# Strassen's derived weight blocks: added up by accumulating transfers from GpSimd, not subtracted by VectorE

## The chip, the cores and the metric

The kernel runs on one core of a Trainium2 chip. A core has five engines that run side by side, each through its own fixed list of instructions: TensorE (PE, matrix products; its weight loads are listed as PEld), VectorE (DVE), ScalarE (ACT), GpSimd (POOL) and SyncE (SP), which here does nothing but issue transfers. Transfers run on 16 DMA engines that all queues of the core share. An instruction that has to wait for a semaphore holds up all that stand behind it on its engine. The metric is the device time of one execution in microseconds (us); lower is better.

## The reference

One layer of a streaming-encoder block on x of 256 tokens by 2048 channels, all in float32. Three sublayers follow one another, each with a layer norm and a conditioning (shift, scale, gate) that is computed from a vector c:

```python
y = _swiglu(modulate(x, 0), ffn1_w13[l], ffn1_w2[l])
x = _layer_norm(ALPHA * x + FFN_WEIGHT * gate[:, 0, None, :] * y, ln_g[l, 0], ln_b[l, 0])
...
x = _layer_norm(ALPHA * x + gate[:, 1, None, :] * y, ln_g[l, 1], ln_b[l, 1])
y = _swiglu(modulate(x, 2), ffn2_w13[l], ffn2_w2[l])
x = _layer_norm(ALPHA * x + FFN_WEIGHT * gate[:, 2, None, :] * y, ln_g[l, 2], ln_b[l, 2])
```

The middle sublayer (an mLSTM beside a gated linear recurrence) is left out here: the change touches only the third, whose SwiGLU is

```python
g, v = jnp.split(u @ w13, 2, axis=-1)
return (jax.nn.silu(g) * v) @ w2
```

with u 256 by 2048, w13 2048 by 2 x 5632 and w2 5632 by 2048.

## The kernel before

**Products in three parts.** A float32 operand is split into a high part (rounded to the matrix unit's format, a cast on ScalarE, L99) and a low part (the rest, a subtraction on VectorE, L101). A product is high x high + low weights x high + high x low, three matmuls (L305, L306, L307) into the same PSUM bank. A weight tile is 128 x 2048 float32, 1 MB; it is loaded by SyncE into one of four buffers of the tag `raw`, and its two parts go into one of three `hi` and three `lo` buffers. In the profile the tiles are called by their first letters: `rw` is the loaded tile of `w2`, `hw` and `lw` its parts; `rf`, `hf`, `lf` the same of `w13`.

**Blocks.** The hidden columns of the feed-forward come in 11 blocks of 512; a block needs `g` (gate) and `v` (value) for two halves t of 128 tokens, over 2048 channels in four tiles of 512. Blocks 4 to 9 of the second feed-forward are *mixed*: two of the four channel tiles (0 and 1) of both `g` and `v` are computed by Strassen's method in Winograd's form. The 2 x 2 blocks of the one operand are token halves by channel tiles, those of the other are the four weight tiles r[0] (`g`, tile 0), r[1] (`v`, tile 0), r[2] (`g`, tile 1) and r[3] (`v`, tile 1). Seven products q1 to q7 take the place of eight, at the price of derived blocks: four of the tokens (`token_sums`, made once), and four of the weights, made in every block by VectorE in place, L880, L881, L882 and L891: r[0] = r[1] - r[0], r[1] = r[3] - r[1], r[3] = r[3] - r[0], r[2] = r[2] - r[3]. Tiles 2 and 3 are multiplied plainly (`plain`).

**The order in a mixed block** is that of `mixed`: q1 (r[0] as loaded), a `w2` tile of the group before, q2 (r[2] as loaded), plain tile 2 of `g`, q3 (r[3] as loaded), a `w2` tile, q6 (r[3] derived), plain tile 3 of `g`, q7 (r[1] derived), a `w2` tile, q5 (r[0] derived), a `w2` tile, q4 (r[2] derived), and the plain tiles of `v`. In the profile `hq` and `lq` are the parts of r[0] to r[3], `m` the PSUM banks of q1, q5, q6 and q7, `fg` and `fv` those of `g` and `v`, `py` those of the `w2` products, `b` the tiles r[0] to r[3] (`b6_3` is r[3] of block 6).

**Buffers.** r[0] and r[1] of every block live in two fixed tiles (tags `scb` and `gate`); r[2] and r[3] take two of the four `raw` buffers, and so the tile that is loaded next into the buffer of r[3] has to wait until r[3] is read for the last time. In blocks 4 to 8 that next tile is the third `w2` tile of the block (`rw22_4_1` in block 6), and in block 9 the fourth. The four tiles of the next block are fetched by `fetch_w` (L835) as their places come free.

**What sets the order.** A scheduler lays the program out on each engine once, when it is built; on the chip every engine keeps to its list. `mov_t` (L298 to L308) issues the products of one token half, `split` (L92) the two parts of a tile.

Of the kernel before, what the change touches and what calls it, by code (L numbers as in the profile page):

```python
# [15 lines left out]
ALU = mybir.AluOpType  # L16
# [38 lines left out]
def block_kernel(ctx: ExitStack, tc: tile.TileContext, a: dict, out: bass.AP):  # L55
    nc = tc.nc
# [16 lines left out]
    def bank(name):  # L73
        return psp.tile([P, 512], F32, tag="ps", name=name)

    def raw_tile(name):
        return wp.tile([P, 2048], F32, tag="raw", bufs=4, name=name)
# [14 lines left out]
    def split(tile, act, low):  # L92

        raw, name, into = tile
        hi, lo = into() if into else [wp.tile([P, 2048], F32R, tag=w, bufs=3, name=w[0] + name) for w in ("hi", "lo")]
        step = 512 if fine[0] else 2048
        cols = [slice(c, c + step) for c in range(0, 2048, step)]
        for w in cols:
            act.copy(cut(hi, w), like(raw[:, w], hi))  # L99
        for w in cols:  # L100
            low.tensor_sub(cut(lo, w), like(raw[:, w], lo), cut(hi, w).bitcast(F32))  # L101
        return hi, lo

    def load_w(src, name, into=None):

        return split(load(src, name, into), nc.scalar, nc.vector)
# [191 lines left out]
    def mov_t(ps, hl, acth, actl, k0, t, first, last, te=nc.tensor, part=slice(0, 512)):  # L298

        hi, lo = hl  # L300
        tk = slice(t * P, (t + 1) * P)
        for j in range(4):
            w = slice(j * 512 + part.start, j * 512 + part.stop)
            o = like(ps[:, part], hi)
            te.matmul(o, acth[:, k0 + j, tk], cut(hi, w), start=first and j == 0, stop=False)  # L305
            te.matmul(o, acth[:, k0 + j, tk], cut(lo, w), start=False, stop=False)  # L306
            mm = te.matmul(o, actl[:, k0 + j, tk], cut(hi, w), start=False, stop=last and j == 3)  # L307
        return mm  # L308
# [7 lines left out]
    def tile_done(mm):  # L316

        for p in pend:
            p[0] -= 1
        while pend and pend[0][0] <= 0:  # L320
            with tc.issue_after(mm.ins):
                pend.pop(0)[1]()
# [260 lines left out]
    def ffn(s, w13, w2, start, following=None):  # L583
# [221 lines left out]
        def token_sums():  # L805

            home = big.tile([P, 2, KT, P], F32R, tag="x", name="sums")
            ah = raw_tile("usum").rearrange("p (k b) -> p k b", k=8)
            nc.vector.tensor_add(ah, uh[:, 0:8, :].bitcast(F32), ul[:, 0:8, :].bitcast(F32))
            a11, a12, a21, a22 = (ah[:, k:k + 4, t * P:(t + 1) * P] for t in range(NT) for k in (0, 4))
            ss = raw_tile("ssum").rearrange("p (k b) -> p k b", k=KT)
            s1, s2, s3, s4 = (ss[:, 4 * i:4 * i + 4, :] for i in range(4))
            nc.vector.tensor_add(s1, a21, a22)
            nc.vector.tensor_sub(s2, s1, a11)  # L820
            nc.vector.tensor_sub(s3, a11, a21)
            nc.vector.tensor_sub(s4, a12, s2)
            sh, sl = home[:, 0], home[:, 1]
            nc.scalar.copy(sh, ss)
            nc.vector.tensor_sub(sl, ss, sh.bitcast(F32))
            parts[:] = sh, sl
# [11 lines left out]
        def mixed(b, ws, more):  # L838

            sh, sl = parts
            r = [held.pop((b, j)) for j in range(4)]  # L850

            def parted(j, nm):
                return split((r[j], f"{nm}{s}_{b}", None), nc.scalar, nc.vector)

            def product(ps, hl, acth, actl, k0, t, first, last):
                tile_done(mov_t(ps, hl, acth, actl, k0, t, first, last))

            def plain(pss, k, at, first, last):
                tile_k = load_w(w13[8 * b + at + k], f"f{s}_{b}{at}{k}")
                for t in range(NT):  # L860
                    mm = mov_t(pss[t], tile_k, uh, ul, 4 * k, t, first[t], last[t])
                tile_done(mm)

            def part_bank(nm):
                return bank(f"{nm}{s}_{b}")

            def half_tile(tag, nm):
                return sm.tile([P, 512], F32, tag=tag, bufs=2, name=f"{nm}{s}{b}")

            sub = nc.vector.tensor_sub  # L870
            add = nc.vector.tensor_add
            p1 = part_bank("m1")
            product(p1, parted(0, "q1"), uh, ul, 0, 0, True, True)
            next(ws)()
            g = [part_bank("fg0"), part_bank("fg1")]
            v = [part_bank("fv0"), None]
            product(g[0], parted(2, "q2"), uh, ul, 4, 0, True, False)
            plain(g, 2, 0, (False, True), (False, False))
            product(v[0], parted(3, "q3"), sh, sl, 12, 0, True, False)
            sub(r[0], r[1], r[0])  # L880
            sub(r[1], r[3], r[1])  # L881
            sub(r[3], r[3], r[0])  # L882
            w0 = half_tile("u", "wa")
            nc.scalar.copy(w0, p1)
            next(ws)()
            p6 = part_bank("m6")
            product(p6, parted(3, "q6"), sh, sl, 4, 0, True, True)
            z0 = half_tile("gy", "za")
            add(z0, w0, p6)
            plain(g, 3, 0, (False, False), (True, False))  # L890
            sub(r[2], r[2], r[3])  # L891
            if more:
                fetch_w(b + 1, 3)
            p7 = part_bank("m7")
            product(p7, parted(1, "q7"), sh, sl, 8, 0, True, True)
            z1 = half_tile("gy", "zb")
            add(z1, z0, p7)
            next(ws)()
            if more:
                fetch_w(b + 1, 1)  # L900
            p5 = part_bank("m5")
            product(p5, parted(0, "q5"), sh, sl, 0, 0, True, True)
            add(z0, z0, p5)
            add(w0, w0, g[0])
            nc.scalar.activation(w0, w0, AF.Silu)
            next(ws)()
            if more:
                fetch_w(b + 1, 0)
            product(g[1], parted(2, "q4"), uh, ul, 4, 1, False, True)
            w1 = half_tile("u", "wb")  # L910
            add(w1, z1, g[1])
            nc.scalar.activation(w1, w1, AF.Silu)
            add(z1, z1, p5)
            v[1] = part_bank("fv1")
            plain(v, 2, 4, (False, True), (False, False))
            if more:
                fetch_w(b + 1, 2)
            plain(v, 3, 4, (False, False), (True, True))
            for t, (w, z) in enumerate(((w0, z0), (w1, z1))):
                add(z, z, v[t])  # L920
                nc.vector.tensor_mul(w, w, z)
            if 4 * b // GRP not in hts:
                new_h(4 * b // GRP)
            later(3, lambda: turn(b, [w0, w1]))
# [524 lines left out]
```

## Time and profile before

| | us |
|---|---|
| median of three runs (lowest, highest) | 1889.85 (1889.34, 1890.07) |
| the profiled execution | 1891.85 |
| its span in the profile | 1890.1 |
| granted TensorE clock over it | 0.995 |
| stretch of the six mixed blocks | about 1376 to 1757 |

The profile shows one execution. Its page gives the busy time of each engine, the chain of work that ended last, groups of instructions by source line with what ended the idle time before them, and the transfers. Other views used below: the busy time of the engines in stretches of the span, the timeline of one engine (start, duration, engine, line, operation, tiles, count, and in brackets the idle time before it with what ended it), and one tile's instructions. A row of SPq is the issue of a transfer; how long the transfer takes until it has landed stands in the view of the transfers.

### The profile page before, as it was taken

How to read it: one execution, taken by the hardware profiler on the slowest of the kernel's cores; microseconds unless marked ns; L12 is line 12 of the kernel's file. 1: busy time of each engine (PE TensorE's matmuls, PEld its weight loads, DVE VectorE, ACT ScalarE, POOL GpSimd, SP SyncE). 2: the span in 40 equal slices, each digit the busy share in tenths (PEclk: the TensorE clock that was granted, in tenths of full speed). 3: DMA queues.
4: the chain of work that ended last, by engine and by line, in shares of the span. 5: the costliest groups of instructions: out<-in, count | busy, mean ns of one | idle time of the engine just before them, and what ended most of it. 6: DMA issues, size and time to landing. Idle time of an engine off the chain costs nothing.

```text
span 1890.1 us, 21168 instructions
## 1 busy us (share of the span) xinstructions
PE 1852.1 (98%) x8483; PEld 1526.3 (81%) x8483; DVE 1541.1 (82%) x1454; ACT 883.8 (47%) x817; POOL 43.1 (2%) x64
## 2 busy tenths in 40 slices
PE   6999999999999999999999999999999999999997
PEld 4888888888888888688888876888888888888886
DVE  7899978888877988898898886677677788778757
ACT  5633434444433335756734346434454454445440
POOL 0000000000000000000000121000000000000000
PEclk8999999999999999999999999999999999999999
DMA  9989887888988897597689575577845654564762
GB/s 363 350 326 361 339 305 292 312 328 335 358 340 336 332 352 267 185 367 283 223 334 363 219 304 224 226 292 264 311 159 197 223 200 178 201 222 156 270 224 85
DMA packets 73490, 520.05 MB, mean 275 GB/s; under 512 B 8576, under 2 KB 8752, under 8 KB 11056
## 3 DMA queue, kind: packets, MB, share of 16 engines
q1 hardware_dynamic: 71136, 511.74, 71.6%
q10 hardware_dynamic: 1728, 3.80, 0.6%
q0 software_dynamic: 528, 3.17, 0.5%
q8 instruction: 66, 1.08, 0.2%
q14 instruction: 32, 0.26, 0.0%
HBM read 514.46 MB, written 4.22 MB: 274 GB/s over the span
## 4 chain that ended last, share of the span: by engine, by line
PE 86%; DVE 6%; ACT 3%; DMA 3%; issue 2%; POOL 0%; DVEq 0%; SPq 0%; ACTq 0%
PE py L306 6%; PE py L305 6%; PE py L307 6%; PE rp L694 5%; PE rp L695 5%; PE fv L305 5%; PE fv L306 5%; PE rp L696 5%; PE fv L307 5%; PE fg L305 4%; PE fg L306 4%; PE fg L307 4%; PE pj L294 4%; PE tl L305 3%; PE tl L306 3%; PE tl L307 3%
## 5 line engine op out<-in xcount | busy, mean ns | idle before, releaser
L189 DVE CUSTOM_DVE_ANT_0 ada<-ada,scb,badac 128x2048 f32<-128x2048 f32 x142 | 332.9, 2345 | 43.8 <-DMA ada<-in_w_ada 43.7
L99 ACT CAST hw<-rw 128x2048 fp32r<-128x2048 f32 x80 | 153.2, 1915 | 180.4 <-PE py L307 79.0
L101 DVE TENSOR_TENSOR lw<-rw,hw 128x2048 fp32r<-128x2048 f32 x80 | 183.0, 2288 | 55.0 <-ACT hw L99 54.9
L307 PE MATMUL py<-hw,htl 128*128 128x512 f32 x512 | 198.9, 389 | 0.0
L306 PE MATMUL py<-lw,hth 128*128 128x512 f32 x512 | 198.9, 389 | 0.0
L99 ACT CAST hra<-rra 128x2048 fp32r<-128x2048 f32 x63 | 120.6, 1916 | 161.8 <-PE rp L696 122.6
L305 PE MATMUL py<-hw,hth 128*128 128x512 f32 x512 | 195.8, 390 | 0.0
L695 PE MATMUL rp<-lra,u 128*128 128x512 f32 x448 | 174.2, 389 | 1.1 <-DVE lra L101 1.1
L696 PE MATMUL rp<-hra,u 128*128 128x512 f32 x448 | 173.6, 389 | 0.0
L694 PE MATMUL rp<-hra,u 128*128 128x512 f32 x448 | 170.7, 392 | 2.4 <-ACT u L262 1.7
L101 DVE TENSOR_TENSOR lra<-rra,hra 128x2048 fp32r<-128x2048 f32 x63 | 144.0, 2286 | 27.7 <-ACT hra L99 27.6
L101 DVE TENSOR_TENSOR lq<-b,hq 128x2048 fp32r<-128x2048 f32 x42 | 96.1, 2288 | 55.0 <-ACT hq L99 55.0
L99 ACT CAST hq<-b 128x2048 fp32r<-128x2048 f32 x42 | 80.4, 1913 | 118.3 <-PE py L307 62.7
L294 PE MATMUL pj<-u,hs 128*128 128x512 f32 x512 | 122.8, 392 | 0.7 <-ACT hs L99 0.7
L307 PEld LDWEIGHTS py<-hw,htl 128*128 128x128 f32 x512 | 96.1, 188 | 20.1
L305 PEld LDWEIGHTS py<-hw,hth 128*128 128x128 f32 x512 | 96.1, 188 | 20.0
L306 PEld LDWEIGHTS py<-lw,hth 128*128 128x128 f32 x512 | 96.1, 188 | 19.6
L294 PEld LDWEIGHTS pj<-u,hs 128*128 128x128 f32 x512 | 94.2, 188 | 19.5 <-ACT hs L99 1.1
L694 PEld LDWEIGHTS rp<-hra,u 128*128 128x128 f32 x448 | 84.0, 188 | 21.1 <-ACT u L262 2.4
L695 PEld LDWEIGHTS rp<-lra,u 128*128 128x128 f32 x448 | 84.1, 188 | 18.5 <-DVE lra L101 1.5
L99 ACT CAST hfv<-rfv 128x2048 fp32r<-128x2048 f32 x31 | 59.3, 1917 | 84.6 <-PE fg L307 63.2
L696 PEld LDWEIGHTS rp<-hra,u 128*128 128x128 f32 x448 | 84.1, 188 | 17.6
(470 smaller groups left out, 4048.8 us busy)
## 6 DMA issues: line engine op xcount, KB each, us to landing
ada<-in_w_ada SPq DMA_DIRECT2D x142, 1024.0 KB, 5.3
rw<-in_w SPq DMA_DIRECT2D x80, 1024.0 KB, 5.3
rra<-in_w_r SPq DMA_DIRECT2D x64, 1024.0 KB, 5.0
rs<-in_w_s SPq DMA_DIRECT2D x32, 1024.0 KB, 6.4
rfg<-in_w SPq DMA_DIRECT2D x31, 1024.0 KB, 5.3
rfv<-in_w SPq DMA_DIRECT2D x31, 1024.0 KB, 5.5
b<-in_w SPq DMA_DIRECT2D x24, 1024.0 KB, 4.8
rf<-in_w SPq DMA_DIRECT2D x24, 1024.0 KB, 4.8
```

Source lines behind the costliest of these rows:

```text
L99: act.copy(cut(hi, w), like(raw[:, w], hi))
L101: low.tensor_sub(cut(lo, w), like(raw[:, w], lo), cut(hi, w).bitcast(F32))
L189: vec.tensor_tensor_reduce(raw, raw, scb, 1.0, badac[:, s, j, kt:kt + 1], ALU.mult, ALU.add, adac[:, s, j, kt:kt + 1])
L294: nc.tensor.matmul(ps, hi[:, w], u2[:, k].rearrange("p w b -> p (w b)"), start=k == 0, stop=False)
L305: te.matmul(o, acth[:, k0 + j, tk], cut(hi, w), start=first and j == 0, stop=False)
L306: te.matmul(o, acth[:, k0 + j, tk], cut(lo, w), start=False, stop=False)
L307: mm = te.matmul(o, actl[:, k0 + j, tk], cut(hi, w), start=False, stop=last and j == 3)
L694: nc.tensor.matmul(pss[t], uh[:, k0 + j, tk], hi[:, w], start=a0 and j == j0, stop=False)
L695: nc.tensor.matmul(pss[t], uh[:, k0 + j, tk], lo[:, w], start=False, stop=False)
L696: mm = nc.tensor.matmul(pss[t], ul[:, k0 + j, tk], hi[:, w], start=False, stop=a1 and j == j0 + nj - 1)
```

## The change

The four derived weight blocks become sums, made in place by transfers that GpSimd issues and that add what they carry to what is in the destination:

- r[0] += the `v` tile 0, read again from memory (before it was r[1] - r[0], with the other sign of r[0]);
- r[1] += the `v` tile 1, read again from memory;
- r[3] += r[0], from one on-chip tile to another;
- r[2] += r[3], likewise.

The transfers into r[0] and r[1] are issued behind q1's product, that into r[3] behind q3, that into r[2] behind the plain tile 3 of `g`: where the subtractions of r[0], r[1] and r[3] stood together behind q3, they now stand apart. To fit the sums, the signs in `token_sums` and in three of the combinations `z0`, `z1` and `w1` change.

```diff
@@ token_sums
-            nc.vector.tensor_add(s1, a21, a22)
+            nc.vector.tensor_sub(s1, a22, a21)
             nc.vector.tensor_sub(s2, s1, a11)
-            nc.vector.tensor_sub(s3, a11, a21)
-            nc.vector.tensor_sub(s4, a12, s2)
+            nc.vector.tensor_add(s3, a11, a21)
+            nc.vector.tensor_add(s4, a12, s2)
@@ mixed
+            def plus(j, src):
+                nc.gpsimd.dma_start(r[j], src, accum_op=ALU.add)
+
             p1 = part_bank("m1")
             product(p1, parted(0, "q1"), uh, ul, 0, 0, True, True)
+            plus(0, w13[8 * b + 4])
+            plus(1, w13[8 * b + 5])
             next(ws)()
...
             product(v[0], parted(3, "q3"), sh, sl, 12, 0, True, False)
-            sub(r[0], r[1], r[0])
-            sub(r[1], r[3], r[1])
-            sub(r[3], r[3], r[0])
+            plus(3, r[0])
...
             plain(g, 3, 0, (False, False), (True, False))
-            sub(r[2], r[2], r[3])
+            plus(2, r[3])
...
-            add(z0, z0, p5)
+            sub(z0, p5, z0)
...
-            add(w1, z1, g[1])
+            sub(w1, g[1], z1)
...
-            add(z1, z1, p5)
+            sub(z1, z1, p5)
```

On VectorE, in block 6 around the derivation of r[3] and r[2], there stood before (`lq32_6` and `lq62_6` are the low parts of q3 and q6, `lw22_5_0` that of a `w2` tile, `htl2` a part of the hidden activations):

```order
L101 TENSOR_TENSOR lq32_6_10706<-b6_3_10397,hq32_6_10705 128x2048
L882 TENSOR_TENSOR b6_3_10397<-b6_3_10397,b6_0_10504 128x2048
L101 TENSOR_TENSOR lw22_5_0_10729<-rw22_5_0_10726,hw22_5_0_10728 128x2048
L638 TENSOR_TENSOR htl2_10181<-th50_10661,hth2_10180 128x4x128
L638 TENSOR_TENSOR htl2_10181<-th51_10668,hth2_10180 128x4x128
L891 TENSOR_TENSOR b6_2_10557<-b6_2_10557,b6_3_10397 128x2048
L101 TENSOR_TENSOR lq62_6_10760<-b6_3_10397,hq62_6_10759 128x2048
```

and now:

```order
L101 TENSOR_TENSOR lq32_6_10708<-b6_3_10397,hq32_6_10707 128x2048
L101 TENSOR_TENSOR lw22_5_0_10729<-rw22_5_0_10726,hw22_5_0_10728 128x2048
L638 TENSOR_TENSOR htl2_10181<-th50_10663,hth2_10180 128x4x128
L638 TENSOR_TENSOR htl2_10181<-th51_10670,hth2_10180 128x4x128
L101 TENSOR_TENSOR lq62_6_10760<-b6_3_10397,hq62_6_10759 128x2048
```

L882 and L891 are gone, and the rest has kept its order; so have ScalarE's rows. GpSimd, which had nothing between the normalisation ahead of this feed-forward and the gate at its end, now has four rows a block; here from the last of that normalisation to block 4 (`ven11` and `rsn11` belong to it), and then those of block 6 with the first of block 7 (in brackets the semaphores that each waits for: DMAHW are transfers issued by SyncE, DMASW those issued by GpSimd):

```order
L124 TENSOR_TENSOR rsp11_8368<-vep11_8366,mhalf_80 128x1 [waits Pool_49]
L874 DMA b4_1_9781<-in_w13_2 128x2048 [waits DMAHW0_49,DMASW3_49]
L124 TENSOR_SCALAR ven11_8396<-tot11_8392 128x1 [waits DVE_49]
L124 TENSOR_TENSOR rsn11_8398<-ven11_8396,mhalf_80 128x1 [waits Pool_49]
L874 DMA b4_0_9775<-in_w13_2 128x2048 [waits DMAHW3_49,DVE_49]
...
L874 DMA b6_1_10450<-in_w13_2 128x2048 [waits DMAHW2_49,DMASW0_49,DVE_49]
L874 DMA b6_0_10504<-in_w13_2 128x2048 [waits DMAHW4_49,DVE_49]
L874 DMA b6_3_10397<-b6_0_10504 128x2048 [waits DMAHW3_49,DMAHW5_49,DMASW7_49,DMAHW7_49,DMASW5_49,DVE_49]
L874 DMA b6_2_10557<-b6_3_10397 128x2048 [waits DMAHW5_49,DMAHW6_49,DMAHW1_49,DMASW6_49]
L874 DMA b7_1_10861<-in_w13_2 128x2048 [waits DMAHW6_49,DMASW4_49,DVE_49]
```

The accumulate into r[1] comes first in every block, and in block 4 it stands ahead of the two small operations of the normalisation. That into r[3] waits for the one into r[0] (DMASW5) and for the q3 split (DVE), that into r[2] for the one into r[3] (DMASW6). On SyncE the rows of block 6 that load the next block's r[3], two `w2` tiles and what follows stood so before:

```order
L835 DMA b7_3_10808<-in_w13_2 128x2048 [waits DMAHW1_49,DVE_49]
L89 DMA rw22_4_1_10831<-in_w2_2 128x2048 [waits DMAHW4_49,DVE_49]
L89 DMA rw22_5_1_10883<-in_w2_2 128x2048 [waits DMAHW5_49,DMAHW2_49,DVE_49]
L835 DMA b7_1_10861<-in_w13_2 128x2048 [waits DVE_49]
L89 DMA rf2_642_10938<-in_w13_2 128x2048 [waits DMAHW4_49,DVE_49]
```

and now:

```order
L835 DMA b7_3_10808<-in_w13_2 128x2048 [waits DMAHW1_49,DVE_49]
L89 DMA rw22_4_1_10831<-in_w2_2 128x2048 [waits DMASW7_49,DMAHW4_49,DMASW6_49,DVE_49]
L89 DMA rw22_5_1_10883<-in_w2_2 128x2048 [waits DMAHW5_49,DMAHW2_49,DVE_49]
L835 DMA b7_1_10861<-in_w13_2 128x2048 [waits DMASW4_49,DVE_49]
L89 DMA rf2_642_10938<-in_w13_2 128x2048 [waits DMAHW4_49,DVE_49]
```

The order is the same, but `rw22_4_1`, which takes the buffer of `b6_3`, now also waits for the accumulates into r[3] (DMASW6) and r[2] (DMASW7), since the latter reads r[3].

## The prediction

> **What bounds the kernel now.** I read the page's first part, then the busy time by stretch over the part of the program that the change touches, and then the timelines of single engines inside one block of it.
>
> ```profile
> span 1890.1 us, 21168 instructions
> PE 1852.1 (98%) x8483; PEld 1526.3 (81%) x8483; DVE 1541.1 (82%) x1454; ACT 883.8 (47%) x817; POOL 43.1 (2%) x64
> ...
> PE 86%; DVE 6%; ACT 3%; DMA 3%; issue 2%; POOL 0%; DVEq 0%; SPq 0%; ACTq 0%
> ```
>
> TensorE is busy 98% of the span and holds 86% of the chain that ended last. That is an average; the change lies in six blocks, so I asked for four stretches of one block's length (columns: stretch, length, PE, PEld, DVE, ACT and POOL busy, clock, DMA share, GB/s).
>
> ```profile
> 1442.50:1506.00 63.50, 63.50 (x286) 52.68 (x285) 52.33 (x36) 31.23 (x20) 0.00 (x0) 1.00 0.54 198
> 1506.00:1569.40 63.40, 63.40 (x286) 52.56 (x285) 52.16 (x36) 31.23 (x20) 0.00 (x0) 1.00 0.54 200
> ...
> sum 253.80, PE 253.80 PEld 210.48 DVE 208.84 ACT 124.94 POOL 0.00; mean PE 63.45 PEld 52.62 DVE 52.21 ACT 31.23 POOL 0.00
> ```
>
> TensorE has no idle time at all here (253.80 of 253.80 us, at granted clock 1.00). VectorE is busy 52.21 of 63.45 us in a block, so it waits 11 us. So nothing that makes VectorE lighter can shorten these blocks. The question is only whether the sums come in time.
>
> **What is removed.** Four subtractions a block (columns: line, engine, tiles, count, total and mean):
>
> ```profile
> L882 DVE TENSOR_TENSOR b<-b,b 128x2048 f32<-128x2048 f32 x6 | 13.8, 2292 | 0.2
> L880 DVE TENSOR_TENSOR b<-b,b 128x2048 f32<-128x2048 f32 x6 | 13.7, 2285 | 0.0
> L881 DVE TENSOR_TENSOR b<-b,b 128x2048 f32<-128x2048 f32 x6 | 13.7, 2282 | 0.0
> L891 DVE TENSOR_TENSOR b<-b,b 128x2048 f32<-128x2048 f32 x6 | 13.7, 2280 | 0.0
> ```
>
> That is 54.9 us of VectorE in 24 instructions, 9.1 us a block. It lies wholly beside TensorE's work: worth 0. The operations whose sign changes keep engine, size and number: 0.
>
> **What is added.** 24 accumulating transfers of 1 MB, issued by GpSimd, which is idle here (0.00 in the stretches). No accumulating transfer stands in this trace, so its price has to be bounded. These rows are near (tile, queue, count, size, median us from issue to landing; the `gateb` group's landing is the last line):
>
> ```profile
> b<-in_w SPq DMA_DIRECT2D x20, 1024.0 KB, 4.8
> ...
> xb<-xd SPq DMA_DIRECT2D x1, 2048.0 KB, 7.8
> ...
> xd<-x SPq DMA_DIRECT2D x1, 2048.0 KB, 11.3
> ...
> gate<-line POOLq DMA_DIRECT2D x1, 1024.0 KB, 8.2
> ...
> DMA to landing us min/median/max: 5.0/5.0/5.0
> ```
> ```profile
> 921.79 0.33 SPq L188 DMA_DIRECT2D ada<-in_w_ada  x1
> ...
> 922.18 0.56 POOL L212 DMA_DIRECT2D gate<-line  x1 [1.66 <-DMA line<-grow]
> ```
>
> A plain load of 1 MB lands in 4.8 us and one of 2 MB in 7.8: 1.8 fixed and 3.0 per MB. The same MB issued by GpSimd took 5.0 (`gateb`), 0.2 more. The one into `gate`, issued 0.4 us after a load (921.79, 922.18), took 8.2, and 2 MB stored among loads took 11.3: company adds 3.2 to 3.5. An accumulate must fetch the destination as well as the source. From below it costs **5.0** (the second fetch hides); with 2 MB fetched **8.0** alone and **11.3** in company; from above **14.3**, if the two fetches and the write follow one another (1.8 + 3 x 3.0 + 0.2) and company adds 3.3. I take the two fetches as the work, so the 2 MB row is nearest: 8.0 alone.
>
> The Trainium skill, "Collectives: The Full Stack", section "The bandwidth ceiling: the fold count and why AG ≠ RS ≠ AR", says that an add inside the transfer is slow for its second source read, at half the rate, and not for the adding. By it the sum below would stand; without the second read (5.0) there would be no stall. No run here shows an accumulate yet.
>
> **Where each of the four lands.** Block 6, VectorE first, then ScalarE, SyncE's queue and TensorE:
>
> ```profile
> 1505.05 2.28 DVE L101 TENSOR_TENSOR lq<-b,hq 128x2048 fp32r<-128x2048 f32 x1
> ...
> 1522.99 2.29 DVE L101 TENSOR_TENSOR lq<-b,hq 128x2048 fp32r<-128x2048 f32 x1 [1.65 <-ACT hq L99]
> 1525.31 2.29 DVE L882 TENSOR_TENSOR b<-b,b 128x2048 f32<-128x2048 f32 x1
> 1527.52 2.28 DVE L101 TENSOR_TENSOR lw<-rw,hw 128x2048 fp32r<-128x2048 f32 x1
> ...
> 1533.12 2.28 DVE L101 TENSOR_TENSOR lq<-b,hq 128x2048 fp32r<-128x2048 f32 x1
> ```
> ```profile
> 1530.15 1.92 ACT L99 CAST hq<-b 128x2048 fp32r<-128x2048 f32 x1 [3.03 <-PE fg L307]
> ...
> 1541.44 1.92 ACT L99 CAST hw<-rw 128x2048 fp32r<-128x2048 f32 x1 [1.26 <-PE m L307]
> ...
> 1554.64 1.91 ACT L99 CAST hq<-b 128x2048 fp32r<-128x2048 f32 x1 [3.53 <-PE py L307]
> ```
> ```profile
> 1479.07 0.33 SPq L835 DMA_DIRECT2D b<-in_w  x1
> ...
> 1529.83 0.33 SPq L835 DMA_DIRECT2D b<-in_w  x1
> 1535.43 2.53 SPq L89 DMA_DIRECT2D rw<-in_w  x2
> ```
> ```profile
> 1538.75 0.39 PE L306 MATMUL m<-lq,sums 128*128 128x512 f32 x1
> ...
> 1549.40 0.39 PE L306 MATMUL py<-lw,hth 128*128 128x512 f32 x1
> ...
> 1557.56 0.39 PE L306 MATMUL py<-lw,hth 128*128 128x512 f32 x1
> ```
>
> *Into `r[0]`*: may start when the q1 split has read it (1505.05 + 2.28 = 1507.33) and is wanted by the next accumulate at 1525.28: 17.9 us, enough even at 14.3. *Into `r[1]`*: its load was issued at 1479.07, tens of us early: hidden.
>
> *Into `r[3]`*: starts when the q3 split has read it, at 1522.99 + 2.29 = 1525.28. VectorE was done with L882 2.3 us later, and the split q6 then waited for TensorE until 1530.15 anyway. The first matmul that needs q6's low half starts at 1538.75. Split high 1.92 and low 2.28 lie between, so the sum must have landed by 1534.55: **9.3 us after its start**. In those us SyncE also loads the next block's `r[3]` (1529.83, some 2 us earlier once L882 no longer precedes the `lw` that frees its buffer), so I take 8.0 + 2.0 = 10.0, between alone and in full company: 0.7 late.
>
> *Into `r[2]`*: starts when the one before has landed. Its own reader, q4's split at 1554.64, has time. But the `w2` tile that SyncE loads at 1535.43 goes into the buffer of `r[3]`, and now also waits until `r[3]` has been read by this transfer. That load lands 4.8 later, is split (1.92 and 2.28), and its low half is used at 1549.40: it must be issued by 1540.40, **15.1 us after 1525.28**. Behind it in SyncE's order stand one more `w2` tile, needed 8.2 us later (1557.56), and the next block's loads; all have more time than this one. With SyncE waiting, nothing runs beside this transfer: 8.0. The two together are 18.0: **2.9 us late**, the 0.7 included. TensorE's order is fixed, so it waits out the whole of it, and the next block's q3 split is tied to TensorE's buffers (the chain `ACT hq <- PE`), so that every block pays anew.
>
> Block 4 has less room:
>
> ```profile
> 1396.97 2.29 DVE L101 TENSOR_TENSOR lq<-b,hq 128x2048 fp32r<-128x2048 f32 x1 [3.14 <-ACT hq L99]
> ...
> 1422.48 0.39 PE L306 MATMUL py<-lw,hth 128*128 128x512 f32 x1
> ```
>
> From 1399.26 to 1422.48 are 23.22 us, against 24.12 in block 6: 0.9 less, so 3.8 late. In block 9 the buffer of `r[3]` goes to the later `w2` tile, 8.2 us more room, and only the 0.7 is left.
>
> One accumulate stands early: that into block 4's `r[1]` is put on GpSimd ahead of two small operations of the normalisation before it.
>
> ```profile
> 1157.83 0.33 SPq L835 DMA_DIRECT2D b<-in_w  x1
> ...
> DMA to landing us min/median/max: 4.8/4.8/4.8
> ```
> ```profile
> 1166.75 0.62 POOL L124 TENSOR_SCALAR ven<-tot 128x1 f32<-128x1 f32 x1 [5.34 <-DVE nbn L124]
> ```
>
> Its tile lands at 1162.63, and the operation behind it starts at 1166.75: 4.1 us of cover, worth 0; without it the normalisation of half the tokens would move by what is missing.
>
> **The sum.** 3.8 + 4 x 2.9 + 0.7 = **16.1 us**. The profiled execution took 1891.85 us (span 1890.1), so it would take 1908.0; the median of the runs is 2.0 lower, so **1906 us** there.
>
> **The rivals.** *Hidden (not slower).* The pair has 15.1 us a block. If both transfers land within 7.5 us each, TensorE never waits, and the time stays 1890. For it: the 5.0 us of `gateb`; and the share that I gave to company is a choice. Against it: 2 MB alone took 7.8. The Trainium skill, "DMA: Bandwidth & Descriptors", section "Anatomy of one DMA — SWDGE (gpsimd) path", gives 2.0 us plus the bytes at 436 GB/s for one issued by GpSimd: 6.8 us, an estimate for 2 MB, 13.6 for the pair, and so no stall. The trace's GpSimd MB took 5.0 where that rule makes 4.4. Chance 20%.
>
> *Slow accumulate.* At 14.3 each the pair takes 28.6: 13.5 late in a block, 14.4 in block 4; block 9 waits 5.3 (28.6 against 15.1 + 8.2): 14.4 + 4 x 13.5 + 5.3 = 73.7, so 1964. For it: the transfers already fill 0.54 of the DMA engines, 34 of 63.45 us, and four accumulates at 6 us of fetching make that 58, so that company is the rule. Against it: only one load falls into the critical 18 us. From 22 us for the pair (7 a block) I count it here. Chance 27%, half of it beyond 1964.
>
> *Faster.* It would need idle time of TensorE that VectorE makes, and the stretches have none: 3%. That the subtractions simply stay is excluded by the built order, which has 24 fewer VectorE rows and 24 more of GpSimd.
>
> **How the numbers follow.** The forecast, a pair between 15.7 and 22 us, has 50%: 1894 to 1927. The range goes down to 1889, which takes in the hidden case, and up to 1970 for the slow one; some 12% is left above it and 4% below. A measurement of this kernel can tell about 0.2% (3.8 us) from no change. The hidden case falls within it except for its edges: same 0.17, faster 0.03, slower 0.80.
>
> **What would show it.** Right: DVE busy falls by 55 us, TensorE gets idle time only in blocks 4 to 9, ended by `lw` L101 and in front of `py`; SyncE's queue waits before that `rw` load for the accumulate into `r[2]`; accumulates that land in 8 to 10 us. Wrong: landings below 7.5 and PE still without idle time (hidden), or landings of 14 and waits in front of `m` from q6 as long as 5 us (slow). A wait of `ven` on GpSimd near 1166 would show the early accumulate mispriced. Landings over 18 us would break the cover of the one into `r[0]` too.

## The result, and the profile after

The changed kernel takes 1904.32 us (median of 4 runs, 1902.31 to 1906.52), the kernel before 1889.96 on the same chip (1889.34 to 1893.35): a ratio of 1.0073, 95% interval 1.0055 to 1.0090. It is slower by 14.4 us; 1906 was forecast. Its profiled execution took 1906.52 us, with a span of 1904.6.

The head of the page of the changed kernel, with the chain's shares by engine:

```profile
span 1904.6 us, 21239 instructions
PE 1858.7 (98%) x8483; PEld 1526.7 (80%) x8483; DVE 1488.5 (78%) x1430; ACT 882.6 (46%) x817; POOL 61.6 (3%) x88
...
PE 67%; DMA 13%; issue 9%; DVE 6%; ACT 4%; POOL 0%; DVEq 0%; SPq 0%; ACTq 0%; POOLq 0%
```

VectorE lost 24 instructions and 52.6 us, and nothing came of it: the span grew. Transfers now hold 13% of the chain that ended last, against 3%. The next view has the busy time of each engine from one q3 split's end to the next, in five blocks (columns as in the prediction's view by stretch):

```profile
1398.98:1464.84 65.86, 63.67 (x281) 51.57 (x280) 42.21 (x29) 29.66 (x18) 3.43 (x5) 1.00 0.83 255
1464.84:1530.29 65.45, 64.32 (x285) 52.48 (x284) 43.41 (x31) 30.90 (x22) 3.43 (x5) 1.00 0.83 257
1530.29:1596.96 66.67, 64.39 (x285) 52.39 (x284) 43.40 (x31) 30.87 (x21) 3.41 (x4) 1.00 0.82 252
1596.96:1664.20 67.24, 64.58 (x285) 52.35 (x284) 43.41 (x31) 30.88 (x21) 3.42 (x5) 1.00 0.81 250
1664.20:1730.50 66.30, 64.39 (x285) 52.48 (x284) 43.40 (x31) 30.87 (x21) 3.43 (x5) 1.00 0.83 254
```

A block took 63.45 us before (253.80 over four). Against 63.45 the five are longer by 2.4, 2.0, 3.2, 3.8 and 2.8: 14.3 of the span's 14.5 us. TensorE, which had no idle time there, now waits; VectorE is down to 43 us a block, and the DMA engines' share is up from 0.54 to 0.82. What TensorE waited for in the six blocks (columns: line, releaser, us in all, times, longest):

```profile
PE py L306 <- DVE lw L101: 6.1, 5, 1.6
PE m L305 <- ACT hq L99: 3.3, 4, 1.1
PE py L305 <- ACT hw L99: 0.7, 1, 0.7
```

Two places. The waits in front of `py`, 6.8 us, are those of the forecast. The 3.3 in front of `m` are not: they belong to the next block's q1. And the landing times in the same part of the program (tile, queue, count, size, median us):

```profile
rw<-in_w SPq DMA_DIRECT2D x23, 1024.0 KB, 7.8
rf<-in_w SPq DMA_DIRECT2D x23, 1024.0 KB, 5.0
b<-in_w SPq DMA_DIRECT2D x20, 1024.0 KB, 9.0
b<-b POOLq DMA_DIRECT2D x12, 1024.0 KB, 7.9
b<-in_w POOLq DMA_DIRECT2D x11, 1024.0 KB, 10.2
```

An accumulate from one tile into another (`b<-b`: into `r[3]` and `r[2]`) takes 7.9 us, one from memory (`b<-in_w` on GpSimd's queue: into `r[0]` and `r[1]`) 10.2. The plain loads beside them grew from 4.8 to 7.8 (`rw`) and 9.0 (`b`).

Block 6 again, in the order GpSimd, SyncE's queue, ScalarE, TensorE:

```profile
1530.29 0.85 POOL L874 DMA_DIRECT2D b<-b  x1 [13.89 <-DVE lq L101]
1538.49 0.85 POOL L874 DMA_DIRECT2D b<-b  x1 [7.36 <-DMA b<-b]
1557.95 0.85 POOL L874 DMA_DIRECT2D b<-in_w  x1 [18.61 <-DMA b<-in_w]
```
```profile
1532.74 0.33 SPq L835 DMA_DIRECT2D b<-in_w  x1
1545.68 1.58 SPq L89 DMA_DIRECT2D rw<-in_w  x2
1548.17 0.33 SPq L835 DMA_DIRECT2D b<-in_w  x1
...
1566.44 0.33 SPq L89 DMA_DIRECT2D rf<-in_w  x1
```
```profile
1538.31 1.91 ACT L99 CAST hq<-b 128x2048 fp32r<-128x2048 f32 x1 [6.46 <-DMA b<-b]
...
1552.54 1.90 ACT L99 CAST hw<-rw 128x2048 fp32r<-128x2048 f32 x1 [7.64 <-DMA rw<-in_w]
...
1574.89 1.91 ACT L99 CAST hf<-rf 128x2048 fp32r<-128x2048 f32 x1 [8.12 <-DMA rf<-in_w]
```
```profile
1554.49 0.73 PE L305 MATMUL py<-hw,hth 128*128 128x512 f32 x2 [0.67 <-ACT hw L99]
1556.82 0.50 PE L306 MATMUL py<-lw,hth 128*128 128x512 f32 x1 [1.59 <-DVE lw L101]
```

Read downwards: the q3 split ends at 1529.99, the accumulate into `r[3]` is issued at 1530.29, and q6's split starts at 1538.31, 8.3 us after the split's end and in time. The one into `r[2]` goes out at 1538.49, and SyncE, which stands in front of the third `w2` tile because that takes the buffer of `r[3]`, may go on at 1545.68: 15.7 us after the q3 split, 0.6 past the limit of 15.1. Then three loads leave together (two `rw`, one `b`), and the first takes 6.8 us to land, not 4.8 (its split starts 6.9 us after the issue). TensorE waits 2.26 us (0.67 + 1.59).

Block 6 is the worst of the five at this place. All of them, in us (how much later TensorE is behind a place than ahead of it, by the starts of the same matmuls before and after):

| block | third `w2` load issued after the q3 split | it lands after | later at `py` | later at `m` |
|---|---|---|---|---|
| 4 | 15.8 | 4.7 | 1.6 | 1.5 |
| 5 | 15.8 | 4.8 | 1.0 | 1.0 |
| 6 | 15.7 | 6.8 | 2.8 | 0.4 |
| 7 | 16.8 | 4.7 | 1.9 | 1.9 |
| 8 | 16.0 | 4.8 | 1.3 | 1.6 |

In four of the five the load lands as fast as the prediction had it, although the next one leaves 0.4 us behind it. In block 6 alone a fetch of instructions (16 KB) starts together with the load, at 1545.7; that this is the reason is likely, and not shown. The last two columns make 8.6 and 6.3 us (added before rounding), more than the rows of waits. A row counts only from the end of the matmul before it, which lasts 0.39 us, while the next one would have started 0.23 us behind its start; and the first matmuls behind a wait start further apart (0.33 us where it was 0.23). TensorE was some 0.6 us ahead at 1376, so the span grew by 14.5.

The `rf` row is the second place. The loads behind SyncE's wait come late, so that the next block's `r[1]` has its tile late, and GpSimd issues that accumulate at 1557.95, into the time of the remaining loads. The plain v tile issued at 1566.44 lands 8.4 us later, its split and q1's behind it are late, and TensorE waits in front of `m`. In block 6 that is 0.4 us and makes no row of its own; in block 7 it reads:

```profile
1645.84 0.50 PE L305 MATMUL m<-hq,u 128*128 128x512 f32 x1 [1.06 <-ACT hq L99]
```

### The profile page after: what moved, and what is told of

Same layout as the page of the kernel before. It is cut to its first block, busy times and chain, and to the rows that moved or that the text cites. A ratio compares the mean times of both kernels' runs of the same rounds, so it can differ in the third digit from the quotient of the medians.

```text
span 1904.6 us, 21239 instructions
## 1 busy us (share of the span) xinstructions
PE 1858.7 (98%) x8483; PEld 1526.7 (80%) x8483; DVE 1488.5 (78%) x1430; ACT 882.6 (46%) x817; POOL 61.6 (3%) x88
## 4 chain that ended last, share of the span: by engine, by line
PE 67%; DMA 13%; issue 9%; DVE 6%; ACT 4%; POOL 0%; DVEq 0%; SPq 0%; ACTq 0%; POOLq 0%
DMA b<-in_w 5%; PE rp L694 5%; PE rp L696 4%; PE rp L695 4%; PE pj L294 4%; PE py L306 4%; PE py L307 3%; PE py L305 3%; PE fv L306 3%; PE fv L307 3%; PE fv L305 3%; PE fg L306 3%; PE fg L305 3%; PE fg L307 3%; DMA b<-b 3%
## 5 line engine op out<-in xcount | busy, mean ns | idle before, releaser
L695 PEld LDWEIGHTS rp<-lra,u 128*128 128x128 f32 x448 | 84.1, 188 | 18.7 <-DVE lra L101 1.5
```

What stands on the lines that cost most here:

```text
L695: nc.tensor.matmul(pss[t], uh[:, k0 + j, tk], lo[:, w], start=False, stop=False)
```

## The experiments

In all of them the theory is the one of the prediction: what costs is the time of the two accumulates one after the other, against the two limits (9.3 us for q6, 15.1 for the third `w2` load). The main rival is that the traffic itself costs, in any place. The ratios are to the kernel before on the same chip; the last columns are TensorE's waits in the six blocks, in us. Times "after the q3 split" count from its end on VectorE, as the limits do.

| kernel | median us | ratio (95%) | in front of `py` | `m` | `fg`, `fv` |
|---|---|---|---|---|---|
| the change | 1904.32 | 1.0073 (1.0055 to 1.0090) | 6.8 | 3.3 | 0 |
| `r[2]` by VectorE | 1890.61 | 1.0004 (0.9995 to 1.0014) | 0 | 0 | 0 |
| `r[3]` by VectorE | 1890.18 | 1.0000 (0.9991 to 1.0010) | 0 | 0 | 0 |
| both by VectorE | 1890.59 | 1.0000 (0.9990 to 1.0009) | 0 | 0 | 0 |
| copies, no adding | 1889.94 | 1.0001 (0.9992 to 1.0010) | 0 | 0 | 0 |
| five accumulates | 1958.56 | 1.0354 (1.0337 to 1.0371) | 0 | 43.7 | 6.0 |
| `r[2]` twice | 1934.59 | 1.0228 (1.0213 to 1.0243) | 10.4 | 7.4 | 6.0 |
| `r[3]` twice | 1945.84 | 1.0292 (1.0276 to 1.0307) | 0 | 30.1 | 6.0 |
| other buffer | 1910.15 | 1.0101 (1.0084 to 1.0119) | 1.7 | 5.3 | 5.0 |
| tile by GpSimd's queue | 1915.95 | 1.0138 (1.0122 to 1.0154) | 13.5 | 0 | 0 |
| `r[1]` later | 1898.87 | 1.0047 (1.0031 to 1.0064) | 6.4 | 0 | 0 |
| half of `r[2]` | 1893.13 | 1.0017 (1.0008 to 1.0027) | 0 | 0.3 | 0 |
| in halves | 1906.79 | 1.0091 (1.0074 to 1.0108) | 1.0 | 2.3 | 7.0 |

### One of the pair, or both, given back to VectorE

```
-            plus(2, r[3])
+            add(r[2], r[2], r[3])
```


> Only the sum into r[2] goes back to VectorE (an addition); the other three stay accumulating transfers. The profile of the change shows the third w2 load of a block issued 15.4 us after the q3 split, behind the accumulate into r[2], and TensorE idle in front of py. Theory (the wait for r[3]'s buffer): the load is then held only by VectorE's addition and the q6 split, which end about 8.0 + 2.3 + 2.3 = 12.6 us after the q3 split, inside the 15.1 us of room; no idle time in front of py, and only the small waits in front of q1's product stay (3.3 us in the profile of the change): 1893 us. Rival 1 (the extra traffic on the DMA engines makes all loads late): a quarter of the traffic is gone, so a quarter of the 14.4 us: 1901. Rival 2 (the accumulate into r[3] is late for q6): nothing gained, 1904.

```
-            plus(3, r[0])
+            add(r[3], r[3], r[0])
```


> Only the sum into r[3] goes back to VectorE; the other three stay accumulating transfers. Theory: the accumulate into r[2] starts 2.3 us after the q3 split and lands some 7.5 us later, at 9.8 of 15.1 us, so the w2 load is held by nothing new; only the waits in front of q1's product stay: 1893 us. Rival 1 (traffic): three quarters stay, 1901. Rival 2 (r[3] late for q6): all gained, 1890.

Both edits together:

> The sums into r[3] and r[2] go back to VectorE; only the two accumulates that read from memory, into r[0] and r[1], stay. Theory: no wait for r[3]'s buffer; what stays is the late plain tile of v at a block's end, which shares the DMA engines with the accumulate into the next r[1], and q1's split behind it: 1893 us. Rival 1 (traffic): half of the added transfers and all of the added reads from memory stay, 1897. Rival 2: 1890.

All three are as fast as the kernel before. The whole stretch of the six blocks in the kernel that adds `r[2]` by VectorE (columns as above):

```profile
1390.00:1757.00 367.00, 366.98 (x1638) 303.51 (x1637) 263.36 (x181) 179.81 (x115) 13.81 (x16) 1.00 0.76 244
```

18 accumulates are left (16 of them in this stretch), the DMA share is 0.76, and TensorE never waits. Its third `w2` load goes out 12.7 us after the q3 split in block 6, that of the second kernel 11.6, both under the limit of 15.1. So either accumulate of the pair may stay; it takes both to lose anything. The misses are small and on one side: a remainder of some 3 us was expected from the traffic of the accumulate into `r[1]`, and there is none. The waits in front of `m` vanish with the late load; they are a consequence of it.

### The same transfers without the adding

```
-                nc.gpsimd.dma_start(r[j], src, accum_op=ALU.add)
+                nc.gpsimd.dma_start(r[j], src)
```


> The 24 transfers stay with their queue, size, order and waits, but copy in place of adding (the derived blocks are left out). Measures what the adding costs. If the second read is what makes them slow: the two on-chip ones land in some 5.0 to 5.5 us in place of 7.2 to 8.0, the pair takes 10.5 of 15.1 us, and TensorE does not wait in front of py: 1890 to 1893 us. If adding costs nothing and the on-chip path or GpSimd's queue is slow: landings of 7 to 8 us as before, 1904.

No loss, with as many transfers from the same queue, in the same order, with the same waits between them. The landings in the six blocks, and the issue of the first of the pair in block 6:

```profile
b<-b POOLq DMA_DIRECT2D x12, 1024.0 KB, 5.2
b<-in_w POOLq DMA_DIRECT2D x11, 1024.0 KB, 5.1
```
```profile
1528.77 0.53 POOL L874 DMA_DIRECT2D b<-b  x1 [17.45 <-DVE lq L101]
```

A copy from tile to tile takes 5.2 us where the accumulate takes 7.9; by these medians adding costs 2.7 us a MB. For the first of the pair alone it is more: 4.4 to 4.6 us in five blocks (5.7 in the other), against 7.9 to 8.0. It is this that makes the pair too long. The Trainium skill, "Collectives: The Full Stack", section "The bandwidth ceiling: the fold count and why AG ≠ RS ≠ AR", has the cause as the second read, for the add of a collective; 2.7 is close to the 3.0 us a MB that a load's bytes take in the trace of before, so the two agree, though no run here shows the read itself.

### More of it: each of the pair twice, and five accumulates

Into `r[3]` twice, with `r[2]` by VectorE, so that only the limit of 9.3 us counts:

```
             plus(3, r[0])
+            plus(3, r[0])
 ...
-            plus(2, r[3])
+            add(r[2], r[2], r[3])
```


> r[0] is accumulated into r[3] twice, one after the other, and r[2] is made by VectorE (the derived blocks are others): 24 MB as in the change. Tests the other limit: the sum in r[3] lands 8.0 + 7.6 = 15.6 us after the q3 split, VectorE's addition comes ahead of q6's low half (2.3 us each), so this is ready at 20.2 where TensorE wants it at 13.5: 6.7 us late in front of q6's product in six blocks, 1930 us. Rival 1 (traffic): 1904.

Into `r[2]` twice:

```
             plus(2, r[3])
+            plus(2, r[3])
```


> r[3] is accumulated into r[2] twice, one after the other (the derived block is another one). With the longer chain the scheduler hands r[3]'s buffer to the fourth w2 tile of a block in place of the third, which TensorE needs 8.2 us later. Theory: r[2] is done 8.0 + 7.4 + 7.4 = 22.8 us after the q3 split, the room is now 15.1 + 8.2 = 23.3, less 2.1 us since the load behind it lands in 6.9 us in place of 4.8: 1.6 us late in five blocks, 1898 us. If the length of the chain counted wherever the buffer goes: 7.4 us more in five blocks, 1941. Rival 1 (traffic): 1908.

Five in a block, so that none into `r[2]` reads `r[3]` and the buffer of `r[3]` comes free early:

```
             plus(3, r[0])
+            plus(2, w13[8 * b + 5])
+            plus(2, r[0])
 ...
-            plus(2, r[3])
```


> The same derived r[2] by two accumulates that don't read r[3]: the v tile 1 from memory, then r[0]; so there are five accumulates a block, 30 MB in all in place of 24, and the w2 load into r[3]'s buffer waits only for the accumulate into r[3] and the q6 split. Theory (the wait for r[3]'s buffer): the load is issued about 8.0 + 4.6 = 12.6 us after the q3 split, of 15.1: 1890 us; if the fifth transfer beside it makes the accumulate into r[3] land later than 9.3 us, q6 waits instead (at 11.3 us: 2 us a block, 1902). Rival 1 (traffic on the DMA engines): 30 of 24 MB, 1908.

With `r[3]` added twice the place of the loss moves to where the prediction's first limit stands. q6's split in block 4, where the q3 split ended at 1396.64, and then two stretches behind the wait (the figure after the five engines is the granted clock):

```profile
1412.28 1.90 ACT L99 CAST hq<-b 128x2048 fp32r<-128x2048 f32 x1 [15.01 <-DMA b<-b]
```
```profile
1414.20:1422.50 8.30, 7.17 (x15) 4.87 (x16) 7.55 (x6) 3.63 (x3) 0.00 (x0) 0.50 0.49 181
1422.50:1430.80 8.30, 8.30 (x38) 6.84 (x38) 4.54 (x4) 4.78 (x4) 0.86 (x1) 1.00 0.91 326
```

The split starts 15.6 us after the q3 split, 6.3 past the limit of 9.3. The waits are 36.1 us, 6.0 a block, close to that. But the time went up by 55.7, where 40 were expected: behind the wait, 5.54 us in this block, the granted clock is 0.50 for 8.3 us, and 15 matmuls start where 38 do at full clock (1.0 us of it is the wait in front of `fg`). TensorE's busy time is 1871.4 us there, 19.3 more than before; the two make the 55.4. This was in no estimate.

Five accumulates were a miss for both sides (1890 or 1902, and 1908, against 1958.56). Freeing the buffer early helped nothing, because the edit laid a second accumulate beside the one into `r[3]`:

```profile
1555.08 1.76 POOL L874 DMA_DIRECT2D b<-b  x2 [8.83 <-DMA b<-in_w]
```
```profile
b<-b POOLq DMA_DIRECT2D x10, 1024.0 KB, 13.0
```

The 13.0 is the median of two unlike groups: in the five blocks whose rows the trace has, the first of the two in flight lands after 8.7 to 11.4 us and the second after 14.7 to 15.7, where one took 7.9. GpSimd had first waited for another one (8.83). In this block the q3 split ended at 1552.71 and q6's started at 1571.43, 18.7 us later and 9.4 past its limit: 49.7 us of waits in the six blocks. So that kernel tells nothing of the buffer.

With `r[2]` added twice the buffer of `r[3]` went to the fourth `w2` tile, which has 8.2 us more: 1898 was expected if that tile's lateness alone counts, 1941 if the length of the chain counts wherever the buffer goes. 1934.59 came, with waits at three places. This suggests that the tile that inherits the buffer is not the only one that counts: SyncE stands still for all that lies behind it, a long time here. The next three runs ask about this.

### Who waits in SyncE's queue

A 64-column accumulate behind the pair, which makes the buffer of `r[3]` go to the fourth tile with the pair's length nearly unchanged:

```
             plus(2, r[3])
+            nc.gpsimd.dma_start(r[2][:, 0:64], r[3][:, 0:64], accum_op=ALU.add)
```


> All of the change, and behind the accumulate into r[2] one more of 64 of its 2048 columns (32 KB; those columns of the derived block are others). It changes which load takes r[3]'s buffer: the fourth w2 tile of a block in place of the third; nothing is made shorter. Theory: r[2] is done some 15.4 + 2.5 = 18 us after the q3 split, the room is 23.3 us: TensorE never waits, 1890 us. Rival 1 (traffic) and any theory in which the accumulates themselves cost the time: 1904 or more.

A miss. The third `w2` tile was to be free, and was not: it now takes the buffer of a plain tile, whose split stands on VectorE behind q6's, and that waits for the accumulate into `r[3]`. SyncE's rows and ScalarE's of that kernel (the q3 split ended at 1534.83):

```profile
1549.76 6.67 SPq L89 DMA_DIRECT2D rw<-in_w  x2
...
1569.81 0.33 SPq L89 DMA_DIRECT2D rf<-in_w  x1
```
```profile
1579.82 1.91 ACT L99 CAST hf<-rf 128x2048 fp32r<-128x2048 f32 x1 [9.69 <-DMA rf<-in_w]
```

It goes out after 14.9 us, so `py` waits little (1.7), but SyncE then stands in front of the fourth tile until after 1556, and the v tile of the block's end lands after 10.0 us: 10.3 us of waits in front of `m` and `fv`. The loss moved from the first place to the second.

To part the two, the waiting tile alone is issued by GpSimd:

```
+            queue[0] = nc.gpsimd
             next(ws)()
+            queue[0] = nc.sync
```
with `queue[0].dma_start(raw, src)` in `load`.

> The third w2 load of each block, which takes the buffer of r[3] and so waits for the accumulate into r[2], is issued from GpSimd's queue instead of SyncE's. Nothing else changes, and the wait itself stays, but SyncE no longer stands in front of it: the loads behind it (the fourth w2 tile, the next block's r[1], the plain v tiles) go out when their own buffers are free. Theory (two parts: the wait of that one tile, and the crowd of late loads behind SyncE): the waits in front of m for ScalarE's hq, 3.3 us in the six blocks of the change, go, the ones in front of py, 6.8 us, stay or shrink since the load no longer lands with two others (6.9 us there, 5 to 6 alone): 1895 to 1900. Rival (only the one tile's lateness counts, and the rest of the loss is made by the transfers' traffic): 1903 to 1905, with the m waits where they were.

Half right. The waits in front of `m` are gone, as expected when SyncE isn't held. But the time is 1915.95: the ones in front of `py` doubled. GpSimd's row of the load in block 6, ScalarE's split, TensorE, and a stretch behind the waits:

```profile
1549.81 0.56 POOL L90 DMA_DIRECT2D rw<-in_w  x1 [6.76 <-DVE yacc L802]
```
```profile
1558.25 1.90 ACT L100 CAST hw<-rw 128x2048 fp32r<-128x2048 f32 x1 [9.66 <-DMA rw<-in_w]
```
```profile
1560.20 0.73 PE L306 MATMUL py<-hw,hth 128*128 128x512 f32 x2 [2.68 <-ACT hw L100]
1562.53 0.80 PE L307 MATMUL py<-lw,hth 128*128 128x512 f32 x1 [1.59 <-DVE lw L102]
```
```profile
1562.00:1570.00 8.00, 7.47 (x22) 5.98 (x23) 6.07 (x5) 2.42 (x2) 0.00 (x0) 0.62 0.92 266
```

The loads that SyncE may now send earlier (1548.47, 1551.87) are under way when the late one starts, and it lands after 8.4 us instead of 6.8; in the other four blocks after 5.1 to 6.2 instead of 4.7 to 4.8. GpSimd also issues it a little later, 16.1 to 17.0 us after the q3 split instead of 15.7 to 16.8. The wait grows to 4.3 us in block 6, and the clock falls behind it (0.62 in the 8 us); in three of the other four blocks it falls to 0.50 for 3.41 us. So this kernel lost 6.7 us more in front of `py` and the time at low clock besides, for the 3.3 us saved in front of `m`.

And the accumulate into `r[1]` moved behind the one into `r[0]`, some 15 us later, with bytes and all else equal:

```
-            plus(1, w13[8 * b + 5])
+            G.dma_start(r[1], w13[8 * b + 5], accum_op=ALU.add)
```
(`G` keeps the instruction at this place of GpSimd's order.)

> The same 24 accumulates, but each into r[1] is put behind the one into r[0] on GpSimd's queue, so that it runs some 15 us later, in the middle of the block, where no late load waits. Theory (the accumulate into the next block's r[1] collides with the loads that SyncE's wait made late, and with the plain v tile that landed in 8.4 us above all): that tile lands in about 5 to 6, the m waits (3.3 us) go, the py waits (6.8) stay: 1899 to 1901. Rival (the late loads are late because of SyncE's wait alone): 1903 to 1906, m waits as before. If two accumulates one behind the other (13 us each where that was seen) hold up the start of the one into r[3], it is slower than 1906.

As the theory had it: 1898.87. The v tile and its split, at the place where the changed kernel has 1566.44 and 1574.89:

```profile
1561.94 0.33 SPq L89 DMA_DIRECT2D rf<-in_w  x1
```
```profile
1566.82 1.91 ACT L99 CAST hf<-rf 128x2048 fp32r<-128x2048 f32 x1 [4.55 <-DMA rf<-in_w]
```

It lands in 4.9 us instead of 8.4, and there is no wait in front of `m`. This is the second part of the loss, some 5 us of the 14.4: an accumulate colliding with the loads that SyncE's wait made late. The first part, in front of `py`, stays at 6.4 us of waits.

### Shorter, and in pieces

Half of the columns of `r[2]` by VectorE:

```
-            plus(2, r[3])
+            nc.gpsimd.dma_start(r[2][:, 0:1024], r[3][:, 0:1024], accum_op=ALU.add)
+            add(r[2][:, 1024:2048], r[2][:, 1024:2048], r[3][:, 1024:2048])
```


> Of the accumulate into r[2] only the first 1024 of 2048 columns stay a transfer; VectorE adds the other half. The pair then takes 8.0 + some 5.0 = 13 us after the q3 split's end, under the limit of 15.1 that the prediction worked out. Theory (it is the limit that counts, not the number of accumulates): no wait in front of py, and none in front of m: 1889 to 1892. Rival (each MB accumulated costs): 20 of 24 MB added stay on the queue, so 12 of the 14.5 us: 1902.

1893.13, with 21 of the 24 MB of accumulates in place (not 20, as the text has it): the profiled execution, 1891.21, has no wait but 0.3 us. GpSimd issues the first of the pair at 1523.97, 0.3 us after the q3 split, and SyncE is free at 1536.95, 13.3 us after it:

```profile
1523.97 0.85 POOL L874 DMA_DIRECT2D b<-b  x1 [14.19 <-DVE lq L101]
```
```profile
1536.95 1.94 SPq L89 DMA_DIRECT2D rw<-in_w  x2
```

It is the length that counts, not the bytes. The interval (1.0008 to 1.0027) still leaves a loss of some 3 us, which the profiled execution, the fastest of the ten, doesn't show; where it lies stays open. The margin is thin: in block 7 of that execution the half took 5.6 us instead of 4.5 to 4.8, and SyncE was free only after 14.2.

The last run keeps all 24 MB and cuts the pair's transfers in two, so that they might overlap:

```
-            plus(3, r[0])
+            for h in (slice(0, 1024), slice(1024, 2048)): nc.gpsimd.dma_start(r[3][:, h], r[0][:, h], accum_op=ALU.add)
 ...
-            plus(2, r[3])
+            for h in (slice(0, 1024), slice(1024, 2048)): nc.gpsimd.dma_start(r[2][:, h], r[3][:, h], accum_op=ALU.add)
```


> The change with nothing given back to VectorE, but the accumulates into r[3] and into r[2] cut into two transfers of 1024 columns each, so that the first half of r[2] can start while the second half of r[3] is still under way. Bytes and orders of all other engines stay. In the kernel that gave half of r[2] to VectorE a transfer of 512 KB landed 4.6 us after its issue and one of 1 MB 7.9. Both halves of r[3] should be in 8 to 9 us after the q3 split, the second half of r[2] starts then and lands 4.6 later: the third w2 load goes out some 13 to 13.5 us after the q3 split, under the limit of 15.1. Theory (the length of the two transfers one after the other, against this limit, is the whole loss; the bytes are free): 1889 to 1893, no wait of more than a few tenths in front of py or m. Rival (the traffic of 24 MB of accumulates itself makes loads late): 1902 to 1906. If two halves in flight at once slow each other so that nothing overlaps: about 1904 too, with the third w2 load 15.4 us after the q3 split.

The third of the outcomes named there. GpSimd, SyncE and ScalarE in block 6, the median landing of all halves, and the landings in block 6 alone (the four halves and one load):

```profile
1528.60 1.73 POOL L886 DMA_DIRECT2D b<-b  x2 [13.89 <-DVE lq L101]
1533.53 0.85 POOL L895 DMA_DIRECT2D b<-b  x1 [3.20 <-DMA b<-b]
1538.88 0.85 POOL L895 DMA_DIRECT2D b<-b  x1 [4.50 <-DMA b<-b]
```
```profile
1544.07 1.41 SPq L89 DMA_DIRECT2D rw<-in_w  x2
```
```profile
1538.69 1.91 ACT L99 CAST hq<-b 128x2048 fp32r<-128x2048 f32 x1 [8.54 <-DMA b<-b]
```
```profile
b<-b POOLq DMA_DIRECT2D x24, 512.0 KB, 7.1
```
```profile
DMA to landing us min/median/max: 4.6/7.9/9.5
```

The first half of `r[2]` does start early, at 1533.53, while the second half of `r[3]` is under way. The 7.1 is again a median of unlike ones: in block 6 the first half of `r[3]` takes 4.6 us, the second, issued 0.5 us behind it, 9.5, and the first half of `r[2]` 7.9, where the single half of `r[2]` in the run above took 4.5 to 4.8 in five blocks. So `r[3]` is complete 2 us later than uncut. SyncE goes on 15.8 us after the q3 split (which ended at 1528.30), no earlier than without the cut, and q6's split starts after 10.4, past the limit of 9.3: the waits are now mostly in front of `fg`, whose split stands behind q6's. Overlapping accumulates gained nothing here. None of the versions beats the kernel before; with TensorE busy all through these blocks there was nothing to win in them.

## Why the prediction was right, point by point

*VectorE's 54.9 us are worth nothing.* Right. Its busy time fell by 52.6 us, and in the kernels that keep part of that relief (both of the pair given back, or one) the time is that of before to 0.1%.

*Price of an accumulate.* Too high, alone and in company. 8.0 was taken for one alone and 10.0 for `r[3]` with a load beside it. From issue to landing `r[3]` took 7.9 to 8.0, with one load issued some 2.5 us behind it, and `r[2]` 6.9 to 7.4, in block 7 8.1. In the kernel that adds into `r[3]` twice, the second accumulate had little beside it and took 6.9 to 7.2 in five blocks (8.1 in the sixth). So the load costs about 0.9 us, not 2.0. With some 0.7 us for issuing and handing over, the pair held SyncE for 15.7 to 16.8 us and not 18.0. Nor was q6 late, so the 0.7 a block that the sum had for that isn't there, nor is block 9's. The bounds (5.0 to 14.3) held for one at a time; the second of two at once went past them (14.7 to 15.7). The rule of the Trainium skill's "DMA: Bandwidth & Descriptors", section "Anatomy of one DMA — SWDGE (gpsimd) path", gave an estimate of 6.8 us for 2 MB and with that a pair inside 15.1; the trace has 6.9 to 7.4 with little beside it and 7.9 beside a load, and the hidden case that followed from the rule did not come.

*The limit for the third `w2` load, 15.1 us.* Right, and the runs enclose it. With loads that land in about 5 us there are no waits in front of `py` where the load goes out 11.5 to 14.2 us after the q3 split, nor at 14.8 (blocks 5 and 7 of the kernel with the other buffer). There is one of 0.18 us at 15.4 (its block 8), and in the change there are 0.74, 0.94 and 1.56 us at 15.8, 16.0 and 16.8 (blocks 5, 8 and 7). Block 4, with its limit of 14.2, waits 0.46 at 14.8 and 1.27 at 15.8. The term that was mis-sized is the pair, so that these blocks are late by less than forecast. In block 6 alone, 10.0 + 8.0 + 4.8 = 22.8 was measured as 15.7 + 6.9 = 22.6: there two errors of size cancel.

*The limit for q6, 9.3 us.* Right: 8.3 gave no wait, 10.4 to 11.2 one of 1.2 on average (in halves, 7.0 in six), 15.6 to 16.7 one of 6.0 (`r[3]` twice), 17.0 to 19.3 one of 8.3 (five, 49.7 in six).

*Behind it in SyncE's order all have more time.* Wrong, and this is the step that the prediction lacked. The loads behind the wait had the time, but they became late together, met the accumulate into the next block's `r[1]`, which the prediction had called hidden, and cost the waits in front of `m`: 3.3 us in rows, 6.3 by the starts of the matmuls. Moving that one accumulate gave some 5 us back.

*2.9 us a block, 3.8 in block 4, 0.7 in block 9.* The kind is right, the size too large: at the place that was forecast TensorE became 1.6 us later in block 4, 1.0 to 2.8 in the next four and not at all in block 9. That is 8.6 us, where the sum has 15.4 for it. The other 6.3 come from the place that was put at nothing. So it is in good part luck that the sum of 16.1 lies within 2 us of the 14.4 measured: the pair was taken 1.2 to 2.3 us too long in every block, and the second place filled the gap.

*The early accumulate into block 4's `r[1]`.* Right: issued at 1162.87, with the normalisation's operation behind it at 1166.23, 0.5 us earlier than before.

*Rivals.* The hidden case fell by the 0.6 to 1.7 us that the pair takes beyond 15.1: at 13.3 us it is nearly true. The slow case is what two accumulates at once make, the second of which took 14.7 to 15.7 us; its price would probably have been higher than the 1964 worked out, since the clock was halved behind waits of 4.65 us and more (`r[3]` twice).

## What to carry to other kernels

Price an accumulating transfer like a transfer of twice its size, and put it against the time until its reader; then ask who waits for the buffer that it reads, because it holds that too, and everything that stands behind that load in its queue, and the loads then leave together, into whatever else is under way. Moving work off an engine that is not the bound is worth nothing, while each new chain of transfers needs slack: here 13.3 us in 15.1 was nearly free, 15.7 to 16.8 cost 14 us.

## What was not expected of the hardware

*A wait can cost more than itself, and it need not be long.* Behind waits of 5.54 us the granted clock was 0.50 for 8.3 us, behind 2.68 + 1.59 us with two matmuls between them 0.62 over 8 us. It also fell behind 0.57 + 1.59 us (tile by GpSimd's queue, block 5) and behind 0.53 + 1.06 us (other buffer, block 4), for 3.41 us each (columns as in the view by stretch):

```profile
1492.96:1496.37 3.41, 3.41 (x9) 2.65 (x8) 3.41 (x4) 2.42 (x2) 0.30 (x1) 0.50 0.72 226
1447.25:1450.66 3.41, 3.41 (x10) 2.63 (x9) 3.41 (x2) 1.03 (x1) 0.87 (x1) 0.50 0.84 308
```

In the changed kernel, after 0.67 + 1.59, it stayed 1.00; so the length alone doesn't decide. The Trainium skill, "TensorE: Matmul & The Clock Gate", section "Part 1: The HAM clock gate (the "warmup" mystery)", says that TensorE's clock halves after an idle window of about 3.4 us and comes back after a busy one. The low stretches of 3.41 us agree with the window's length, but no whole window of idling was needed here: 1.6 and 2.2 us, each in two pieces with two matmuls between, were enough. What decides it stays open.

*Accumulates gain nothing by overlapping.* The second of two at once landed after 14.7 to 15.7 us, and halves in flight together took up to 9.5 in block 6 instead of 4.6; cut or whole, the pair held SyncE until 15.7 us or more after the q3 split.

*GpSimd needs longer to issue one:* 0.85 us, against 0.53 for the same transfer as a copy and 0.56 for a plain load.
